# First weight blocks of the MLPs requested ahead of the output projections, second matmul's first transfers behind them, and two ordering choices undone

## The chip, the cores and the metric

The kernel runs on one core of a Trainium2 chip. The core has five engines that run side by side and meet at semaphores: PE (TensorE, matrix products; PEld is its loading of the stationary operand), DVE (VectorE), ACT (ScalarE), POOL (GpSimd) and SP (SyncE, which here only issues DMA transfers). Transfers between the main memory and the on-chip memory are issued by SP and, where they accumulate into their target, by POOL; each of the two issues in the order of its own queue. The metric is the device time of one execution in microseconds (us).

## The reference: what is computed

Two encoder layers on x of 512 tokens by 1024 features, float32. Each layer is a token mixer and a dense MLP, each behind an RMS norm and added to the residual:

```python
def sq_relu_mlp(h, w1, w2):
    a = jax.nn.relu(h @ w1)
    return (a * a) @ w2
...
for i in range(DEPTH):                        # DEPTH = 2
    h = rms_norm(x, norm_mix[i])
    y = dilated_mixer(h, ...) if i % 2 == 0 else mla_mixer(h, ...)   # each ends with  o @ w_o
    x = x + y
    h = rms_norm(x, norm_ffn[i])
    x = x + sq_relu_mlp(h, ffn_w1[i], ffn_w2[i])
```

w1 is 1024 by 4096 and w2 is 4096 by 1024. The mixer of layer 1 is a dilated window attention with a joint q/k/v projection, that of layer 2 a latent attention over all positions. Both end with an output projection w_o of 1024 by 1024.

## The kernel before

**Arithmetic.** Float32 operands are split into a rounded high part and a remainder (ACT writes `whi`, DVE subtracts and writes `wlo`), and each product is three matmuls: high by high, high by low, low by high. The large matmuls save products in the manner of Strassen and Winograd: a 2 by 2 block product takes seven products, numbered 1 to 7, of sums and differences of blocks.

**The MLP.** `mlp` works in eight groups of 512 columns of w1 (class `Up`, first matmul) and four chunks of 1024 rows of w2 (`wino`, reached by `down(ch)`, second matmul). A group has four weight blocks of 512 KB. The first, key (0, 0), goes to a tile with the tag `wk` (two slots) when the `Up` is made. `rest()` loads the other three into tiles with the tag `raw` (three slots, which the output projection's weights use as well). `product(p)` makes the high and low part of its weight operand in slots `whi` and `wlo` (four each) and issues 24 matmuls of 128 by 256 at L968. Products 5 and 6 add another block to the first one on DVE (L936, L938). Products 7 and 4 need blocks that an accumulating DMA on POOL has added to (`load(..., add=True)`, L922). The blocks of the normalised activations are written by `project`, in `hT_f` (`H` in `Up`; the order in it is `H_OF`).

`wino` first runs `fetch` for four pairs of half blocks into `wqs`: eight plain loads on SP (L788) and four accumulations on POOL (L786); this is its first `next(d)`. `wqs` takes the place of the attention output that the projection reads. In `mlp` the sequence is: group 0's loads, its products 1 and 2, group 1's product 1, group 0's products 5, 6, 3, 7, 4, group 1's loads and its products 5, 6, 3, 7, 2, 4; then for each chunk the `plan`, in which a 0 stands for `next(d)` and another number for a product of the current group.

**The output projection and the norm.** `project` multiplies the attention output by w_o in two column halves (`run_block` at L185, weights loaded at L147 and split at L157 and L158), adds to the residual (L1077), normalises each of four row tiles (L137, L1051), transposes it on PE (L124) and writes the blocks of `hT_f` with ACT and DVE (L1042, L1043, and sums at L1064 to L1071). It runs in a pool `po` (or `po1`), which is closed before the MLP's pool is opened; `hT_f` stands in an outer pool (`h1`, `bh`).

**Order.** A planner sets the order of the instructions on each engine from the order in which they are written, their dependencies and its own estimate of times, so that a transfer can go ahead of work written before it. `tc.issue_after(ins)` holds everything written in its block behind `ins` on the engine of `ins`. Pools with `reuse_waits="tile"` share memory with closed pools, and a new tile waits for the release of the tiles whose place it takes.

**Two other places.** `v_phase` does the v projection of layer 1 by seven products for each of three head groups. Its `piece(g, ba)` needs the sum bT + b21 for product 4; for g = 0 it is formed by two accumulating DMAs that read the weights again (L464), for the others by `add_block` on DVE (L334). `wq` has six slots for these blocks. In layer 2 the attention runs over four pairs of heads; `score` notes the maximum and the exponential of each step, and the splits of the second w_o on DVE and ACT are held behind the first step of the last pair.

Of the kernel before, what the change touches and what calls it, by code (L numbers as in the profile page):

```python
# [10 lines left out]
F32 = mybir.dt.float32  # L11
# [6 lines left out]
P = 128  # L18
# [69 lines left out]
def encoder_kernel(ctx: ExitStack, tc: tile.TileContext, x, norm_mix, norm_ffn, a_w_qkv, a_q_gain, a_k_gain,  # L88
# [218 lines left out]
    def v_phase(vp):  # L307
# [139 lines left out]
        def piece(g, ba):  # L447

            bb = new_banks("b")
            both(5, bT[g], bb, True)  # L450
            put(g, 1, 1, "set", bb, False)
            add_block(bT[g], bT[g], b22[g])
            both(3, b22[g], bb, False)
            put(g, 0, 1, "set", bb, False)
            b3 = vp.tile([P, 4, VH], F32, tag="h32", name=nm("b3"))
            add_block(b3, b12[g], b22[g])
            both(6, bT[g], ba, False)
            put(g, 0, 1, "sub", ba, True)
            if g:
                add_block(bT[g], bT[g], b21[g])  # L460
            else:

                for u in range(2):
                    nc.gpsimd.dma_start(bT[g][:, 2 * u:2 * u + 2], wblk(g, 1, 0, u), accum_op=ALU.add)  # L464
# [300 lines left out]
    def wino(tag, Aq, w, wqs, asps, pool, resid, done=None):  # L765
# [28 lines left out]
        def sums(p, t):  # L794

            if p == 7:
                if done is None:
                    d = gp.tile([P, 4, 256], F32, tag="gain", name=nm("d"))
                else:
                    d = pool.tile([P, 4, 256], F32, tag="wk", name=nm("d"), bufs=2)  # L800
                V.tensor_tensor(d, Aq(0, 0), Aq(1, 0), op=ALU.subtract)
                split_to(t, d)
            elif p == 6:
                split_to(t, S["d"])
            else:
# [99 lines left out]
    class Up:  # L905
# [3 lines left out]

        CHAIN = {1: "a", 6: "a", 7: "a", 4: "a", 5: "b", 3: "b", 2: "d"}  # L910

        def __init__(self, w1, c0, H, a2, pool):
            self.v = w1.rearrange("(k p) c -> p k c", p=P)
            self.c0, self.H, self.a2, self.banks = c0, H, a2, {}
            self.w = {(0, 0): self.load((0, 0), pool.tile([P, 4, 256], F32, tag="wk", name=nm("wk"), bufs=2))}

        def load(self, key, t, add=False):

            ki, ni = key
            src = self.v[:, 4 * ki:4 * ki + 4, self.c0 + 256 * ni:self.c0 + 256 * ni + 256]  # L920
            if add:
                nc.gpsimd.dma_start(t, src, accum_op=ALU.add)  # L922
            else:
                nc.sync.dma_start(t, src)
            return t

        def rest(self):
# [55 lines left out]
                V.tensor_tensor(c, c, av, op=op)  # L983
                self.end(c, c)

    def mlp(layer, w1, w2, H, resid, pool, done):
        wqs = big.tile([P, 8, 2, 512], F32, tag="hT", name=nm("wqs"))
        asps = pool.tile([P, 2, 4, 2, 256], F32R, name="asp")
        a2c = pool.tile([P, 4, S], F32, name="a2")
# [2 lines left out]
        homes = [a2ab[:, 0], a2ab[:, 1], a2c]  # L992

        def group(h):
            return Up(w1, 512 * h, H, homes[h % 3], pool)

        def down(ch):
            a2s = [homes[(2 * ch + j) % 3] for j in range(2)]
# [2 lines left out]
                        done if ch == 3 else None)  # L1001


        g0 = group(0)
        g0.rest()
        g0.product(1)
        g0.product(2)
        g1 = group(1)
        g1.product(1)
        for p in (5, 6, 3, 7, 4):  # L1010
            g0.product(p)
# [5 lines left out]
        for ch in range(3):  # L1017
            d = down(ch)
            for h, plan in ((2 * ch + 2, (0, 1, 5, 0, 6, 3, 0, 7, 2, 0, 4, 0, 0)),
                            (2 * ch + 3, (1, 5, 6, 0, 3, 7, 2, 0, 4))):  # L1020
                g = group(h)
                g.rest()
                for p in plan:
                    if p:
                        g.product(p)
                    else:
                        next(d)
        for _ in down(3):
# [62 lines left out]
    h1p = tc.tile_pool(name="h1p", bufs=1, reuse_waits="tile")  # L1091
    h1 = h1p.__enter__()
    hT = h1.tile([P, 7, 4, 2, 256], F32R, name="hT_f0")
    with tc.tile_pool(name="po", bufs=1, reuse_waits="tile") as po:
        project(oA, a_w_o[0], resid, norm_ffn[0:1, :].rearrange("o d -> (o d)"), hT, po, "g_ffn0",
                first_cols)
    with tc.tile_pool(name="mlp0", bufs=1, reuse_waits="tile") as mp:
        state = {}

        def done0(r, c):  # L1100
            state[r] = state.get(r, 0) + 1
            if state[r] < 2:
# [10 lines left out]
    if True:  # L1113
        with tc.tile_pool(name="bpool", bufs=1, reuse_waits="tile") as bp, \
# [153 lines left out]
            def score(d, h, r):  # L1268
# [6 lines left out]
                for i, (lt, rt) in enumerate(ops):  # L1275
                    PE.matmul(sc, lhsT=lt, rhs=rt, start=(i == 0), stop=(i == 4))  # L1276
                mx = st.tile([P, 4], F32, tag="bmx", name=nm("bmx"))
                marks["max"] = V.tensor_reduce(mx[:, 0:1], sc, axis=AX.X, op=ALU.max).ins
                V.tensor_scalar(mx[:, 1:2], mx[:, 0:1], rq, -1.0, op0=ALU.mult, op1=ALU.mult)
                pe = bw.tile([P, S], F32, tag="pe", name=nm("pe"), bufs=3)  # L1280
                marks["exp"] = A.activation(pe, sc, AF.Exp, bias=mx[:, 1:2], scale=rq, accum_out=mx[:, 2:3]).ins
# [41 lines left out]
            for s_ in range(HB * NT + lag):  # L1323
                p, c = divmod(s_, 8)
                if s_ < HB * NT:
                    if c == 0 and p:
                        cur = nxt
                    pend.append((cur, c // 4, c % 4, score(cur, c // 4, c % 4)))
                    if s_ == HB * NT - 8:
                        last_pair = marks["max"], marks["exp"]  # L1330
                if s_ >= lag:
                    d, h2, r2, f = pend.pop(0)
                    if r2 == 0:
# [17 lines left out]

    bh = ctx.enter_context(tc.tile_pool(name="bh", bufs=1, reuse_waits="tile"))
    hT = bh.tile([P, 7, 4, 2, 256], F32R, name="hT_f1")

    with tc.tile_pool(name="po1", bufs=1, reuse_waits="tile") as po, \
            tc.issue_after(last_pair[0]), tc.issue_after(last_pair[1]):
        project(oB, b_w_o[0], resid, norm_ffn[1:2, :].rearrange("o d -> (o d)"), hT, po, "g_ffn1")
    with tc.tile_pool(name="mlp1", bufs=1, reuse_waits="tile") as mp:
        mlp(1, ffn_w1[1], ffn_w2[1], hT, resid, mp, lambda r, c: nc.sync.dma_start(
            out_v[:, r, 512 * c:512 * c + 512], resid[:, r, 512 * c:512 * c + 512]))  # L1360


# [30 lines left out]
```

## Time and profile before

| | us |
|---|---|
| median of 3 runs | 1465.89 (1465.11 to 1466.90) |
| the profiled execution's own time | 1464.43 |
| its span (first to last instruction) | 1462.7 |
| PE busy | 1380.8 (94%) |
| DVE busy | 1079.1 (74%) |
| ACT busy | 825.0 (56%) |
| POOL busy | 259.0 (18%) |

The mean granted clock of TensorE is 0.979 of full speed. The rows that the next part shows are of a few kinds. A row of the timeline has the start in us, the duration, the engine, the line of the kernel, the operation, the tile written and the tiles read, their sizes and the count of instructions; in square brackets stands how long the engine was idle before it and what ended that. A row of the waits has the waiting engine and tile, what it waited for, the total in us, the number of times and the longest. A row of the chain of work that ended last has the start, the duration and what. A row of windows has the stretch, its length, then the busy time of each engine with the number of its instructions, the granted clock, the mean busy share of the DMA engines and GB/s.

### The profile page before, as it was taken

The page shows a single profiled execution, that of the slowest core. Times are in us where ns is not written, and L with a number is a line of the kernel's source. Part 1 is how long each engine was busy: PE and PEld are TensorE (multiplying, and loading weights), DVE is VectorE, ACT ScalarE, POOL GpSimd, SP SyncE. Part 2 cuts the span into 40 slices and gives each one's busy share as a digit, 9 for nine tenths or more (in the row PEclk, how much of TensorE's full clock was granted, in tenths as well). Part 3 has the DMA queues.
Part 4 walks back from the last instruction along what each step waited for, and adds up shares of the span by engine and source line. Part 5 has one row for each costly group of instructions (what it writes and reads, how often), then busy time and mean ns, then how long its engine had stood idle before and what let it go on. Part 6 is the DMA issues. An engine that isn't in the chain of part 4 may idle for free.

```text
span 1462.7 us, 21731 instructions
## 1 busy us (share of the span) xinstructions
PE 1380.8 (94%) x8004; PEld 1216.5 (83%) x8004; DVE 1079.1 (74%) x1691; ACT 825.0 (56%) x1730; POOL 259.0 (18%) x274
## 2 busy tenths in 40 slices
PE   7999999999999994999999998999895899999998
PEld 7998888888889983999999886777664898999886
DVE  6886758776787646687878787797746687888876
ACT  5554556454665524665656554776524565656663
POOL 1211112011121001121112121433201111221210
PEclk9999999999999996999999998999998899999999
DMA  9635222323222338788988862200115779889855
GB/s 320 191 118 177 86 75 89 97 87 114 82 83 67 99 113 230 169 187 207 194 212 184 198 144 55 80 30 1 58 58 161 159 185 209 195 191 217 182 130 115
DMA packets 154922, 202.98 MB, mean 139 GB/s; under 512 B 8960, under 2 KB 108544, under 8 KB 154816
## 3 DMA queue, kind: packets, MB, share of 16 engines
q1 hardware_dynamic: 118192, 144.96, 31.0%
q0 software_dynamic: 36624, 56.63, 22.8%
q8 instruction: 63, 1.03, 0.3%
q14 instruction: 43, 0.35, 0.1%
HBM read 193.70 MB, written 7.86 MB: 138 GB/s over the span
## 4 chain that ended last, share of the span: by engine, by line
PE 82%; DMA 7%; DVE 4%; issue 3%; ACT 3%; SPq 1%; POOL 0%; ACTq 0%; DVEq 0%; POOLq 0%
PE acc L185 27%; PE acc L968 19%; PE sc L885 11%; PE tp L885 7%; PE tp L124 3%; DMA wk<-in_ffn_w_dram 3%; PE sc L421 2%; DMA wqs<-in_ffn_w_dram 2%; PE acc L1300 1%; PE acc L1276 1%; PE sc L1194 1%; PE tp L421 1%; PE sco L706 1%; PE sc L592 1%; PE sco L702 1%
## 5 line engine op out<-in xcount | busy, mean ns | idle before, releaser
L185 PE MATMUL acc<-whi,hT 128*128 128x512 f32 (+2 forms) x1216 | 384.2, 390 | 2.2 <-ACT hT L744 1.3
L968 PE MATMUL acc<-hT_f,whi 128*128 128x256 f32 x1792 | 329.0, 286 | 33.8 <-ACT whi L954 32.9
L968 PEld LDWEIGHTS acc<-hT_f,whi 128*128 128x128 f32 x1792 | 285.5, 194 | 39.0 <-ACT whi L954 34.3
L185 PEld LDWEIGHTS acc<-whi,hT 128*128 128x128 f32 x1216 | 225.9, 188 | 41.9 <-ACT hT L744 1.9
L968 PE MATMUL acc<-hT_f,wlo 128*128 128x256 f32 x896 | 254.4, 285 | 0.0
L185 PE MATMUL acc<-wlo,hT 128*128 128x512 f32 (+2 forms) x608 | 235.9, 388 | 0.1
L968 PEld LDWEIGHTS acc<-hT_f,wlo 128*128 128x128 f32 x896 | 173.4, 194 | 0.0
L885 PE MATMUL sc<-whi,asp 128*128 128x512 f32 x512 | 164.4, 392 | 3.2 <-ACT asp L762 2.0
L823 DVE TENSOR_TENSOR wlo<-wqs,whi 128x1024 fp32r<-128x1024 f32 x112 | 136.4, 1228 | 32.4 <-ACT whi L822 32.1
L822 ACT ACTIVATE whi<-wqs 128x1024 fp32r<-128x1024 f32 x112 | 118.2, 1055 | 73.2 <-PE acc L968 37.4
L158 DVE TENSOR_TENSOR wlo<-raw,whi 128x1024 fp32r<-128x1024 f32 (+3 forms) x82 | 94.3, 1160 | 55.5 <-ACT whi L157 55.3
L786 POOL DMA_DIRECT2D wqs<-in_ffn_w_dram x64 | 77.2, 1208 | 319.6 <-DMA wqs<-in_ffn_w_dram 166.8
L185 PEld LDWEIGHTS acc<-wlo,hT 128*128 128x128 f32 x608 | 114.4, 188 | 18.9 <-DVE wlo L158 0.4
L885 PEld LDWEIGHTS sc<-whi,asp 128*128 128x128 f32 x512 | 96.9, 189 | 24.5 <-ACT asp L762 4.7
L157 ACT ACTIVATE whi<-raw 128x1024 fp32r<-128x1024 f32 (+3 forms) x82 | 82.3, 1009 | 57.8 <-PE acc L185 21.9
L885 PE MATMUL tp<-whi,asp 128*128 128x512 f32 x352 | 112.3, 390 | 0.0
L132 POOL TENSOR_TENSOR qrs<-rs_v,nhalf 128x4 f32<-128x4 f32 x48 | 59.3, 1241 | 288.2 <-DVE rs_v L129 239.4
L955 DVE TENSOR_TENSOR wlo<-wk,whi 128x1024 fp32r<-128x1024 f32 x64 | 78.2, 1224 | 38.6 <-ACT whi L954 38.3
L954 ACT ACTIVATE whi<-wk 128x1024 fp32r<-128x1024 f32 x64 | 67.6, 1059 | 67.7 <-DMA wk<-in_ffn_w_dram 30.2
L885 PE MATMUL sc<-wlo,asp 128*128 128x512 f32 x256 | 100.6, 393 | 0.0
L137 ACT ACTIVATE junk<-acc 128x128 f32<-128x128 f32 x192 | 53.2, 277 | 56.8 <-PE acc L185 51.8
L955 DVE TENSOR_TENSOR wlo<-raw,whi 128x1024 fp32r<-128x1024 f32 x48 | 58.6, 1224 | 34.7 <-ACT whi L954 32.4
(258 smaller groups left out, 2604.3 us busy)
## 6 DMA issues: line engine op xcount, KB each, us to landing
wqs<-in_ffn_w_dram SPq DMA_DIRECT2D x80, 512.0 KB, 5.0
wqs<-in_ffn_w_dram POOLq DMA_DIRECT2D x64, 512.0 KB, 6.4
raw<-in_a_w_qkv_dram SPq DMA_DIRECT2D x96, 256.0 KB, 3.2
raw<-in_ffn_w_dram SPq DMA_DIRECT2D x48, 512.0 KB, 5.7
b<-in_a_w_qkv_dram SPq DMA_DIRECT2D x24, 384.0 KB, 5.8
wk<-in_ffn_w_dram SPq DMA_DIRECT2D x16, 512.0 KB, 6.8
raw<-in_ffn_w_dram POOLq DMA_DIRECT2D x16, 512.0 KB, 6.5
wk<-in_ffn_w_dram POOLq DMA_DIRECT2D x16, 512.0 KB, 7.6
```

The costliest lines, as they stand in the source:

```text
L132: G.tensor_tensor(out, v[:, :n], nhalf[:, :n], op=ALU.pow)
L137: A.activation(junk, x, AF.Square, scale=1.0 / math.sqrt(dim), accum_out=out)
L157: A.activation(hi[:, :nk, :n], raw[:, :nk, :n], AF.Copy)
L158: V.tensor_tensor(lo[:, :nk, :n], raw[:, :nk, :n], hi[:, :nk, :n].bitcast(F32), op=ALU.subtract)
L185: PE.matmul(accs[o][:, oc], lhsT=lt, rhs=rt, start=(kt == 0 and p_i == 0 and hv == 0), stop=(kt == total - 1 and p_i == 2), skip_group_che ...
L786: marks["sum"] = nc.gpsimd.dma_start(t, src, accum_op=ALU.add).ins
L822: A.activation(hi, x, AF.Copy)
L823: V.tensor_tensor(lo, x, hi.bitcast(F32), op=ALU.subtract)
L885: PE.matmul(bk[t], lhsT=lt, rhs=rt[:, j], start=(first and k == 0 and i_ == 0), stop=(k == 3 and i_ == 2), skip_group_check=True)
L954: A.activation(hi, x, AF.Copy)
L955: V.tensor_tensor(lo, x, hi.bitcast(F32), op=ALU.subtract)
L968: PE.matmul(acc[:, 256 * o:256 * o + 256], lhsT=lt, rhs=rt, start=(first and o == 0 and k == 0 and i_ == 0), stop=(o == 1 and k == 3 and i ...
```

## The change

1. `Up` is made before `project` for groups 0 and 1 of each MLP, with `wk` in the outer pool, so that the two (0, 0) blocks are requested ahead of the output projection. `wk` of the later groups, and `xn` of the next layer's norm, use the same tiles.
2. The first `next(d)` of chunk 0, which issues the eight plain `wqs` loads, is held on SP behind group 1's last plain load.
3. In the last chunk of layer 1 the difference tile of product 7 moves from a `wk` slot to a `raw` slot.
4. In `v_phase`, g = 0 forms its sum with `add_block` like the others.
5. The splits of the second w_o are no longer held behind the last attention pair.

```diff
@@ piece
-            if g:
-                add_block(bT[g], bT[g], b21[g])
-            else:
-                for u in range(2):
-                    nc.gpsimd.dma_start(bT[g][:, 2 * u:2 * u + 2], wblk(g, 1, 0, u), accum_op=ALU.add)
+            add_block(bT[g], bT[g], b21[g])
@@ wino, sums
-                    d = pool.tile([P, 4, 256], F32, tag="wk", name=nm("d"), bufs=2)
+                    d = wp.tile([P, 2, 512], F32, tag="raw", name=nm("d"), bufs=3).rearrange(
+                        "p k (h n) -> p (k h) n", h=2)
@@ Up
-        def __init__(self, w1, c0, H, a2, pool):
+        def __init__(self, w1, c0, H, pool, a2=None):
...
-                nc.sync.dma_start(t, src)
+                self.last = nc.sync.dma_start(t, src).ins
@@ mlp
-    def mlp(layer, w1, w2, H, resid, pool, done):
+    def mlp(layer, w1, w2, H, resid, pool, hpool, g0, g1, done):
...
-            return Up(w1, 512 * h, H, homes[h % 3], pool)
+            return Up(w1, 512 * h, H, hpool, homes[h % 3])
...
-        g0 = group(0)
+        g0.a2, g1.a2 = homes[:2]
         g0.rest()
         g0.product(1)
         g0.product(2)
-        g1 = group(1)
         g1.product(1)
...
-                for p in plan:
+                for n, p in enumerate(plan):
                     if p:
                         g.product(p)
+                    elif h == 2 and n == 0:
+                        with tc.issue_after(g1.last):
+                            next(d)
                     else:
                         next(d)
@@ layer 1
     hT = h1.tile([P, 7, 4, 2, 256], F32R, name="hT_f0")
+    g0, g1 = (Up(ffn_w1[0], 512 * h, hT, h1) for h in range(2))
     with tc.tile_pool(name="po", bufs=1, reuse_waits="tile") as po:
         project(oA, a_w_o[0], resid, ...)
...
-            norm_tile(r, resid[:, r], state["g"], state["hT"], mp, xn_tag="wk")
-        mlp(0, ffn_w1[0], ffn_w2[0], hT, resid, mp, done0)
+            norm_tile(r, resid[:, r], state["g"], state["hT"], h1, xn_tag="wk")
+        mlp(0, ffn_w1[0], ffn_w2[0], hT, resid, mp, h1, g0, g1, done0)
@@ layer 2 (the notes of max and exp in score, and last_pair, go)
     hT = bh.tile([P, 7, 4, 2, 256], F32R, name="hT_f1")
-    with tc.tile_pool(name="po1", bufs=1, reuse_waits="tile") as po, \
-            tc.issue_after(last_pair[0]), tc.issue_after(last_pair[1]):
+    g0, g1 = (Up(ffn_w1[1], 512 * h, hT, bh) for h in range(2))
+    with tc.tile_pool(name="po1", bufs=1, reuse_waits="tile") as po:
         project(oB, b_w_o[0], resid, ...)
...
-        mlp(1, ffn_w1[1], ffn_w2[1], hT, resid, mp, lambda r, c: ...)
+        mlp(1, ffn_w1[1], ffn_w2[1], hT, resid, mp, bh, g0, g1, lambda r, c: ...)
```

More of the change, by code (lines that the diff above doesn't have):

```diff
@@ L1277, in score @@
                 mx = st.tile([P, 4], F32, tag="bmx", name=nm("bmx"))
-                marks["max"] = V.tensor_reduce(mx[:, 0:1], sc, axis=AX.X, op=ALU.max).ins
+                V.tensor_reduce(mx[:, 0:1], sc, axis=AX.X, op=ALU.max)
                 V.tensor_scalar(mx[:, 1:2], mx[:, 0:1], rq, -1.0, op0=ALU.mult, op1=ALU.mult)
                 pe = bw.tile([P, S], F32, tag="pe", name=nm("pe"), bufs=3)
-                marks["exp"] = A.activation(pe, sc, AF.Exp, bias=mx[:, 1:2], scale=rq, accum_out=mx[:, 2:3]).ins
+                A.activation(pe, sc, AF.Exp, bias=mx[:, 1:2], scale=rq, accum_out=mx[:, 2:3])
                 V.reciprocal(mx[:, 3:4], mx[:, 2:3])
@@ L1328, in encoder_kernel @@
                     pend.append((cur, c // 4, c % 4, score(cur, c // 4, c % 4)))
-                    if s_ == HB * NT - 8:
-                        last_pair = marks["max"], marks["exp"]
                 if s_ >= lag:
@@ L1353, in encoder_kernel @@
     hT = bh.tile([P, 7, 4, 2, 256], F32R, name="hT_f1")
-    with tc.tile_pool(name="po1", bufs=1, reuse_waits="tile") as po, \
-            tc.issue_after(last_pair[0]), tc.issue_after(last_pair[1]):
+    g0, g1 = (Up(ffn_w1[1], 512 * h, hT, bh) for h in range(2))
+    with tc.tile_pool(name="po1", bufs=1, reuse_waits="tile") as po:
         project(oB, b_w_o[0], resid, norm_ffn[1:2, :].rearrange("o d -> (o d)"), hT, po, "g_ffn1")
     with tc.tile_pool(name="mlp1", bufs=1, reuse_waits="tile") as mp:
-        mlp(1, ffn_w1[1], ffn_w2[1], hT, resid, mp, lambda r, c: nc.sync.dma_start(
+        mlp(1, ffn_w1[1], ffn_w2[1], hT, resid, mp, bh, g0, g1, lambda r, c: nc.sync.dma_start(
             out_v[:, r, 512 * c:512 * c + 512], resid[:, r, 512 * c:512 * c + 512]))
```

## The prediction

> **What bounds the kernel now.** I read the page first, then the list of waits, the PE rows around the longest waits, and the DMA queue of SP.
>
> ```profile
> span 1462.7 us, 21731 instructions
> PE 1380.8 (94%) x8004; PEld 1216.5 (83%) x8004; DVE 1079.1 (74%) x1691; ACT 825.0 (56%) x1730; POOL 259.0 (18%) x274
> L968 PE MATMUL acc<-hT_f,whi 128*128 128x256 f32 x1792 | 329.0, 286 | 33.8 <-ACT whi L954 32.9
> ```
>
> PE (TensorE) is busy 94% of the span, so 82 us of it is idle at most. The last line is the first matmul of the MLPs: of 33.8 us of idle time before its 1792 instructions, 32.9 wait for one thing, the rounded weight `whi` that ACT makes at L954. The waits say how often, and what ACT waited for:
>
> ```profile
> PE acc L968 <- ACT whi L954: 32.9, 4, 17.3
> ACT whi L954 <- DMA wk<-in_ffn_w_dram: 30.2, 8, 8.3
> ```
>
> Four waits, the longest 17.3 us: two large ones, one per MLP. The PE rows on both sides of them:
>
> ```profile
> 552.92 1.14 PE L124 MATMUL tp<-ck,xn 128*128 128x128 f32 x8 [2.26 <-ACT h L1059]
> ...
> 555.86 1.93 PE L124 MATMUL tp<-ck,xn 128*128 128x128 f32 x8 [1.79 <-DVE dif L1065]
> 575.13 0.79 PE L968 MATMUL acc<-hT_f,whi 128*128 128x256 f32 x2 [17.34 <-ACT whi L954]
> ...
> 595.21 0.50 PE L968 MATMUL acc<-hT_f,whi 128*128 128x256 f32 x2 [0.21 <-ACT a L977]
> ...
> 1119.48 1.94 PE L124 MATMUL tp<-ck,xn 128*128 128x128 f32 x8 [1.79 <-DVE dif L1065]
> 1136.71 0.80 PE L968 MATMUL acc<-hT_f,whi 128*128 128x256 f32 x2 [15.29 <-ACT whi L954]
> ...
> 1157.93 0.51 PE L968 MATMUL acc<-hT_f,whi 128*128 128x256 f32 x2 [0.67 <-ACT a L977]
> ```
>
> The last transposes of the normalisation end at 557.8 and 1121.4; then PE stands still for 17.34 and 15.29 us. Why is in SP's queue:
>
> ```profile
> 511.42 1.50 SPq L924 DMA_DIRECT2D raw<-in_ffn_w_dram  x2
> 549.82 4.09 SPq L788 DMA_DIRECT2D wqs<-in_ffn_w_dram  x8
> 554.25 2.76 SPq L924 DMA_DIRECT2D wk<-in_ffn_w_dram  x2
> 577.50 11.49 SPq L924 DMA_DIRECT2D raw<-in_ffn_w_dram  x3
> ...
> 1049.49 10.70 SPq L147 DMA_DIRECT2D raw<-in_b_w_o_dram  x5
> 1113.44 3.96 SPq L788 DMA_DIRECT2D wqs<-in_ffn_w_dram  x8
> 1117.50 3.15 SPq L924 DMA_DIRECT2D wk<-in_ffn_w_dram  x2
> ```
>
> `wk`, the block that the first product needs, is asked for at 554.25 and 1117.50, right behind eight `wqs` transfers for the second matmul. The chain that ended last names the same two tiles:
>
> ```profile
> 553.43 13.73 DMA wqs<-in_ffn_w_dram
> ...
> 1118.63 21.74 DMA wk<-in_ffn_w_dram
> ```
>
> **The change part by part.** *First blocks early (both MLPs).* Four `wk` transfers (two groups, two MLPs) move ahead of the output projection. They take no engine time but SP's issue, under 0.5 us each. What it removes is the PE gap, and the slow clock behind it:
>
> ```profile
> 575.00:580.00 5.00, 4.71 (x21) 4.42 (x22) 0.52 0.55 149
> 580.00:590.00 10.00, 10.00 (x86) 10.00 (x85) 1.00 0.60 112
> ```
>
> These are windows over L968 alone (length, PE busy and its matmuls, PEld, granted clock, DMA share, GB/s). After the gap the granted clock is 0.52, then 1.00: 21 matmuls take the 4.87 us from 575.13 to 580, and 21 at the later rate (10/86 = 0.116 us) take 2.43. So 2.4 us more is lost per gap. The Trainium skill, "TensorE: Matmul & The Clock Gate", Part 1, says that an idle TensorE falls to half rate and needs some 3.4 us of sustained work to come back. The trace agrees (0.52 against 1.00); by the page the loss would be an estimated 1.7 us per gap, and the sum 1.4 us smaller.
>
> Gone with the wait: 17.3 + 2.4 + 0.2 (the wait at 595.21) = 19.9 us in the first MLP, 15.3 + 2.4 + 0.7 = 18.4 in the second (its slow start taken as in the first).
>
> *What is late next: DVE.* In the same stretch DVE still builds the blocks of the normalised activations:
>
> ```profile
> 549.80:567.00 17.20, 3.94 (x24) 3.02 (x22) 14.50 (x23) 10.19 (x18) 4.24 (x4) 0.68 0.97 298
> 565.74 0.69 DVE L1043 TENSOR_TENSOR hT_f<-dif,hT_f 128x512 fp32r<-128x512 f32 x1 [0.70 <-ACT hT_f L1042]
> 584.19 1.22 DVE L955 TENSOR_TENSOR wlo<-wk,whi 128x1024 fp32r<-128x1024 f32 x1
> ```
>
> DVE is busy 14.50 of the 17.20 us up to 567 (third figure with a count), so 2.7 us are free, and its last block (row at 565.74) ends at 566.4. Products 1 and 2 of group 0 and 1 of group 1 need only blocks of the first two row tiles. They are 3 x 24 matmuls x 0.12 = 8.6 us and carry PE from 557.8 to 566.4. By then DVE must also have done three low parts (row at 584.19, 1.22 us), and for product 5 an addition and a low part of the same size: 6.1 us in 2.7 free ones. So product 5 starts between 566.4 and 566.4 + 3.4 = 569.8; with no row for the order, I take the middle: 1.7 us of new wait. Product 4 needs a DMA accumulation issued after product 6's split; before the change product 7 began 595.21 - 585.41 = 9.8 us after that split and three products hide 8.6, so 0 to 2 us, I take 1. Left: 17.2 and 15.7, together 32.9 us, between 38.3 (no new wait) and 27.5 (both waits at their worst, in both MLPs).
>
> *Second matmul's transfers behind group 1's last load.* The added edge binds only SP's eight `wqs` loads; POOL's four accumulations follow their data. Before the change group 1's loads were issued 577.50 to 589.0, some 14 us after the first product; so afterwards about 560 to 574, and `wqs` from 574. Queued behind it on SP: group 2's blocks. The first product of the second matmul comes after 16 products, 46 us, near 604, so `wqs` has 30 us, and its own lateness costs nothing. But between 560 and 606 the DMA engines must now move 23 transfers of 512 KB (3 of group 1, 8 `wqs`, 4 of group 2, 8 accumulations): 12.1 MB in 46 us, 262 GB/s. Compare:
>
> ```profile
> 575.00:606.00 31.00, 30.50 (x234) 30.01 (x235) 22.31 (x21) 19.41 (x26) 5.15 (x4) 0.92 0.68 143
> raw<-in_ffn_w_dram POOLq DMA_DIRECT2D x16, 512.0 KB, 6.5
> 594.16 1.28 POOL L922 DMA_DIRECT2D raw<-in_ffn_w_dram  x1 [7.17 <-DVE wk L936]
> L954 ACT ACTIVATE whi<-wk 128x1024 fp32r<-128x1024 f32 x64 | 67.6, 1059 | 67.7 <-DMA wk<-in_ffn_w_dram 30.2
> ```
>
> Before the change that stretch ran at 143 GB/s, because the gap had taken the `wqs` traffic; the 298 GB/s at 0.97 share above is near the ceiling. Group 1's first accumulation was issued at 594.16; 6.5 us to land and 2.3 to split (1.06 + 1.22) make it ready at 603, and the product that needs it came five products after 595.2, at 609.6: 6.6 us of slack. Bounds: 0, or 6.5 us per MLP if POOL holds one behind a `wqs` accumulation (rival 1). I take 2 per MLP, nearer 0, since the demand is under the rate shown: 4 us back. The Trainium skill, "DMA: Bandwidth & Descriptors", section "Queues, rings and completion order", says that each DMA engine takes turns between the queues by packet, so a POOL accumulation would not wait out SP's backlog. By that the 4 us would be about 0; no row here separates the two.
>
> *The v stage's block sum on DVE again.* Two accumulating DMAs leave POOL's queue, two DVE additions come.
>
> ```profile
> 51.40 1.23 POOL L464 DMA_DIRECT2D bT<-in_a_w_qkv_dram  x1 [1.37 <-DVE wlo L407]
> 59.25 0.84 ACT L406 ACTIVATE whi<-bT 128x768 fp32r<-128x768 f32 x1 [3.63 <-DMA bT<-in_a_w_qkv_dram]
> 60.88 0.62 PE L421 MATMUL acc<-whi,hT 128*128 128x384 f32 x2 [1.49 <-ACT whi L406]
> 51.62 1.82 DVE L334 TENSOR_TENSOR bT<-b,b 128x768 f32<-128x768 f32 x2
> ```
>
> PE loses 1.49 us to that DMA. The additions cost DVE 1.82 (last row, the same form), in place of that very row: b21 now lives until the additions are done, so the next b11 lands in its slot later and the sum of b11 and b12 at 51.62 must move back. Gain 1.5; if instead the late b11 or DVE holds PE, a loss of up to 1.9. I take the gain, as the DMA wait has its own row.
>
> *The edge on the last attention pair taken back.* The splits of the second w_o may go ahead of the last pair's first maximum and exponential.
>
> ```profile
> 1047.15 2.95 ACT L157 ACTIVATE whi<-raw 128x1024 fp32r<-128x1024 f32 x3
> 1047.31 1.59 PE L1276 MATMUL sc<-kn,qn 128*128 128x512 f32 x3 [2.77 <-ACT pe L1281]
> ```
>
> Earlier splits would let projection matmuls fill the 2.77 us hole (+2.8) or put 2.95 us of ACT work in the way of the softmax (-3.0). I take 0. The difference tile in `raw` and the new home of `xn` change slots that are free by then: 0.
>
> **Sum.** 32.9 - 4.0 + 1.5 = 30.4. The profiled execution took 1464.43 (span 1462.7), so 1434.0; the median of runs is 1.5 above it, so 1435.5 us. Differences under 0.2% (2.9 us) could not be told from none.
>
> **Rivals.**
> 1. *POOL in order.* If the planner sets the `wqs` accumulation before group 1's, POOL waits for its data: six transfers (3.1 MB at 298 GB/s, 10.6 us) after 574, so to 585, two issues of 1.2, then 6.5 to land and 2.3 to split: 596, against a need at 591 (eight products after product 5 at 568.1). With group 1's second accumulation behind it and DVE at its bound, 6 to 7 us per MLP more than I took: 1448. For: the 13.73 us row of `wqs`. Against: from 595 on PE shows no such wait, with the same mix on POOL.
> 2. *Everything fits.* Product 1 also fills the holes before the last transposes (2.26 + 1.79, taken alike in both MLPs: 8.1), no new wait, no crowding: 38.3 + 8.1 + 1.5 + 2.8 = 50.7, 1415. Against: DVE's 14.50 of 17.20.
> 3. *It doesn't do what it says.* `wk` stays late because its place is taken until the projection ends. By the tile sizes it lies behind 56 KB of hT_f, over qkT in layer 1 and vb in layer 2:
>
> ```profile
> L592 PE MATMUL sc<-qkT x32: 270/275/275, 462.5 to 487.0; 128*128 128x128 f32 x32
> 1082.92 3.70 PE L1300 MATMUL tp<-pTs,vb 128*128 128x512 f32 x8 [0.69 <-ACT pTs L1292]
> ```
>
> These end at 487 and 1086.6, 70 and 35 us before the gaps, so little speaks for it: 1464.
>
> 4. *Slower: SP held by the early request.* SP issues in order. Were `wk` set ahead of the five w_o loads of 1049.49, it would hold them until vb is free at 1086.6: 37 us of the second projection, and 1435.5 + 37 = 1472. It decides once the hold passes 30 us. Against: the planner let `raw` go before `wk` at 511.42.
>
> **How the numbers follow.** My forecast 0.57 (its own range 1427 to 1442), rival 1 0.20, rival 2 0.12, rival 3 0.05, rival 4 0.06. The range goes from 1418 (half of rival 2's way) to 1451 (rival 1 with its bounds) and leaves out rivals 3, 4 and part of 2. Faster 0.89, within 0.2% 0.05, slower 0.06.
>
> **What would show it.** Right: no PE wait above 3 us before L968; SP's `wk` rows before the projections' end and `wqs` behind `raw`; a granted clock of 1.0 where 0.52 stood; the first L885 matmul some 17 us nearer to the last transpose. Wrong: waits of PE on `whi` in group 1 with POOL rows idle on DMA wqs (rival 1), or SP idle on PE ahead of L147 (rival 4). The v step is right if the 1.49 us before 60.88 is gone and none came at the next group's start.

## The result and the profile after

The changed kernel takes 1444.62 us (median of 4 runs, 1444.02 to 1446.12), the kernel before 1465.5 beside it (4 runs): the ratio is 0.986, with a 95% interval of 0.984 to 0.988. The gain is 20.9 us; 30.4 were forecast. In the kernel after, L968 has become L964, L954 and L955 are L950 and L951, L885 is L881, L788 and L786 are L783 and L781, L922 and L924 are L918 and L920, and the parts of `hT_f` written at L1042 (ACT) and L1043 (DVE) are now written at L1041 and L1042. The experiments shift the lines again: L966 and L973 below are the same matmul as L964.

The page of the kernel after, its first lines and the group of the MLP's first matmul:

```profile
span 1442.9 us, 21746 instructions
PE 1382.1 (96%) x8004; PEld 1219.4 (85%) x8004; DVE 1081.0 (75%) x1693; ACT 823.3 (57%) x1730; POOL 256.3 (18%) x272
L964 PE MATMUL acc<-hT_f,whi 128*128 128x256 f32 x1792 | 337.9, 290 | 25.6 <-ACT whi L950 12.0
```

PE's work is the same (1382 us), the span 19.8 us shorter. The wait on `whi` has shrunk from 32.9 us to 12.0 and has not gone, and the same 1792 matmuls take 337.9 us where they took 329.0: more of them run at a low clock. PE's rows with a wait above 1 us, first MLP and then second (timeline, in brackets the wait and what ended it):

```profile
553.93 0.58 PE L964 MATMUL acc<-hT_f,whi 128*128 128x256 f32 x1 [2.08 <-DVE hT_f L1042]
568.01 0.38 PE L964 MATMUL acc<-hT_f,whi 128*128 128x256 f32 x1 [2.57 <-ACT hT_f L1041]
569.81 0.38 PE L964 MATMUL acc<-hT_f,whi 128*128 128x256 f32 x1 [1.41 <-DVE hT_f L1042]
607.21 0.80 PE L964 MATMUL acc<-hT_f,whi 128*128 128x256 f32 x2 [6.83 <-ACT whi L950]
609.26 0.58 PE L964 MATMUL acc<-hT_f,wlo 128*128 128x256 f32 x1 [1.25 <-DVE wlo L951]
...
1101.46 0.39 PE L964 MATMUL acc<-hT_f,whi 128*128 128x256 f32 x1 [2.59 <-DVE hT_f L1042]
1115.74 0.38 PE L964 MATMUL acc<-hT_f,whi 128*128 128x256 f32 x1 [2.45 <-ACT hT_f L1041]
1117.51 0.58 PE L964 MATMUL acc<-hT_f,whi 128*128 128x256 f32 x1 [1.39 <-DVE hT_f L1042]
1154.21 0.80 PE L964 MATMUL acc<-hT_f,whi 128*128 128x256 f32 x2 [5.20 <-ACT whi L950]
1156.26 0.58 PE L964 MATMUL acc<-hT_f,wlo 128*128 128x256 f32 x1 [1.25 <-DVE wlo L951]
```

The 17.34 us hole is gone: the first products run from 550.87 us on, between the transposes. The two shorter holes ahead of the transposes (2.26 and 1.79 us) are gone with it. In their place stand two kinds of waits. Three of 1.4 to 2.6 us are for parts of `hT_f`: the one at 553.93 for the second row tile, whose transposes start at 549.58, the two from 565.4 on for the last one, whose transposes end at 564.0. The other kind is one of 6.83 and 1.25 us (5.20 and 1.25 in the second MLP) in group 1, at product 4. The queues show why. SP, then POOL in the first MLP, then the chain that ended last:

```profile
514.95 1.05 SPq L920 DMA_DIRECT2D wk<-in_ffn_w_dram  x2
529.07 40.48 SPq L920 DMA_DIRECT2D raw<-in_ffn_w_dram  x4
569.95 6.85 SPq L783 DMA_DIRECT2D wqs<-in_ffn_w_dram  x8
...
1069.63 0.92 SPq L920 DMA_DIRECT2D wk<-in_ffn_w_dram  x2
```

```profile
592.57 1.18 POOL L781 DMA_DIRECT2D wqs<-in_ffn_w_dram  x1 [9.51 <-DMA wqs<-in_ffn_w_dram]
593.27 1.80 POOL L918 DMA_DIRECT2D wk<-in_ffn_w_dram  x1
```

```profile
575.34 16.69 DMA wqs<-in_ffn_w_dram
...
593.27 11.86 DMA wk<-in_ffn_w_dram
...
605.16 1.06 ACT whi L950
```

SP does what the change says: `wk` at 514.95, `wqs` behind group 1's last load. On POOL an accumulation of `wqs` stands idle 9.51 us for a plain load that took 16.69 us to land, and the accumulation into `wk` that product 4 needs stands behind it in order. Issued at 593.27, it lands 11.86 us later. The clock after such waits, in windows over L964 alone (length, PE, PEld, granted clock, DMA share, GB/s), and a window over all engines for the transfers:

```profile
570.00:575.00 5.00, 5.00 (x31) 5.00 (x31) 0.66 0.85 263
607.00:612.00 5.00, 3.54 (x15) 3.25 (x16) 0.50 0.35 107
```

```profile
576.00:607.00 31.00, 24.39 (x202) 24.08 (x201) 11.68 (x12) 13.27 (x18) 6.10 (x5) 0.96 1.09 273
```

### The profile page after: what moved, and what is told of

It is laid out like the page before. It is cut to its first block, busy times and chain, and to the rows that moved or that the text cites. A ratio compares the mean times of both kernels' runs of the same rounds, so it can differ in the third digit from the quotient of the medians.

```text
span 1442.9 us, 21746 instructions
## 1 busy us (share of the span) xinstructions
PE 1382.1 (96%) x8004; PEld 1219.4 (85%) x8004; DVE 1081.0 (75%) x1693; ACT 823.3 (57%) x1730; POOL 256.3 (18%) x272
## 4 chain that ended last, share of the span: by engine, by line
PE 81%; DVE 7%; DMA 5%; issue 3%; ACT 2%; SPq 1%; POOL 0%; DVEq 0%; ACTq 0%; POOLq 0%
PE acc L185 25%; PE acc L964 18%; PE sc L881 11%; PE tp L881 8%; PE tp L124 4%; DMA wqs<-in_ffn_w_dram 3%; PE sc L421 3%; DMA wk<-in_ffn_w_dram 2%; PE acc L1300 1%; PE acc L1276 1%; PE sc L1194 1%; PE tp L421 1%; DVE wlo L951 1%; PE sco L701 1%; PE sc L587 1%
## 5 line engine op out<-in xcount | busy, mean ns | idle before, releaser
L964 PE MATMUL acc<-hT_f,whi 128*128 128x256 f32 x1792 | 337.9, 290 | 25.6 <-ACT whi L950 12.0
L964 PEld LDWEIGHTS acc<-hT_f,whi 128*128 128x128 f32 x1792 | 291.4, 198 | 31.5 <-ACT whi L950 12.4
L964 PE MATMUL acc<-hT_f,wlo 128*128 128x256 f32 x896 | 257.4, 289 | 2.5 <-DVE wlo L951 2.5
L964 PEld LDWEIGHTS acc<-hT_f,wlo 128*128 128x128 f32 x896 | 176.4, 197 | 3.1 <-DVE wlo L951 3.1
L881 PE MATMUL sc<-whi,asp 128*128 128x512 f32 x512 | 163.4, 390 | 4.5 <-DVE resid L849 2.5
L781 POOL DMA_DIRECT2D wqs<-in_ffn_w_dram x64 | 77.6, 1213 | 334.4 <-DMA wqs<-in_ffn_w_dram 185.3
L881 PEld LDWEIGHTS sc<-whi,asp 128*128 128x128 f32 x512 | 96.2, 188 | 25.6 <-ACT asp L757 6.1
L951 DVE TENSOR_TENSOR wlo<-wk,whi 128x1024 fp32r<-128x1024 f32 x64 | 78.3, 1223 | 46.1 <-ACT whi L950 45.8
L881 PE MATMUL tp<-whi,asp 128*128 128x512 f32 x352 | 112.3, 390 | 0.0
L950 ACT ACTIVATE whi<-wk 128x1024 fp32r<-128x1024 f32 x64 | 67.5, 1058 | 65.0 <-DMA wk<-in_ffn_w_dram 23.9
L881 PE MATMUL sc<-wlo,asp 128*128 128x512 f32 x256 | 99.9, 390 | 0.0
L951 DVE TENSOR_TENSOR wlo<-raw,whi 128x1024 fp32r<-128x1024 f32 x48 | 58.8, 1225 | 36.9 <-ACT whi L950 34.5
```

The lines of the kernel that those rows point to most:

```text
L781: marks["sum"] = nc.gpsimd.dma_start(t, src, accum_op=ALU.add).ins
L881: PE.matmul(bk[t], lhsT=lt, rhs=rt[:, j], start=(first and k == 0 and i_ == 0), stop=(k == 3 and i_ == 2), skip_group_check=True)
L950: A.activation(hi, x, AF.Copy)
L951: V.tensor_tensor(lo, x, hi.bitcast(F32), op=ALU.subtract)
L964: PE.matmul(acc[:, 256 * o:256 * o + 256], lhsT=lt, rhs=rt, start=(first and o == 0 and k == 0 and i_ == 0), stop=(o == 1 and k == 3 and i ...
```

## Where the 20.9 us come from

The same instruction's time in the trace before less that in the trace after places the gain. At the first matmul of `wino` (L885 and L881; 624.1 and 620.2) it is 3.9 us. At product 7's first matmul in the first MLP's last chunk (894.0 and 880.9) it is 13.1. At the first and the last L1300 of attention B it is 11.9 and 17.0 (the last at 1086.0 and 1069.0), and at the second MLP's first `wino` matmul (1186.8 and 1166.8) 20.0. So the two MLP starts, forecast at 32.9, give 3.9 and 3.0, and the rest comes from two places that were costed at nothing: the end of the first MLP (9.2) and attention B (5.1); 1.2 are lost between them.

The end of the first MLP, in PE and DVE of the kernel before, then of the kernel after:

```profile
888.76 1.97 PE L124 MATMUL tp<-ck,xn 128*128 128x128 f32 x8 [5.62 <-DVE xn L220]
891.15 1.22 DVE L801 TENSOR_TENSOR d<-a 128x1024 f32<-128x1024 f32 x1
894.02 1.23 DVE L763 TENSOR_TENSOR asp<-d,asp 128x1024 fp32r<-128x1024 f32 x1 [0.25 <-ACT asp L762]
```

```profile
876.71 1.22 DVE L758 TENSOR_TENSOR asp<-d,asp 128x1024 fp32r<-128x1024 f32 x1
880.94 0.47 PE L881 MATMUL sc<-whi,asp 128*128 128x512 f32 x1 [1.26 <-DVE resid L849]
```

Before, product 7's operand is split at 894.02, since its difference tile waited for a `wk` slot that the next layer's normalised tiles held; PE meanwhile ran their transposes after 5.62 us of standing. After, its last part is made from 876.71 to 877.9, 3 us ahead of the matmul.

## The experiments

All times are medians; the kernel before was run beside each group of them (1464.95 to 1466.94).

**The changed kernel again**, unchanged, as a base for what is changed in it.

> The changed kernel itself, beside the three that follow, so that differences of a few microseconds can be read. 1444.6 us, 0.986 of the kernel before.

Measured: 1444.61 us.

**`wqs` behind product 4's accumulation.** The order of rival 1, turned round: group 1's second accumulation now goes ahead of `wqs`.

```diff
-                nc.gpsimd.dma_start(t, src, accum_op=ALU.add)
+                self.acc = nc.gpsimd.dma_start(t, src, accum_op=ALU.add).ins
...
-                        with tc.issue_after(g1.last):
+                        with tc.issue_after(g1.last), tc.issue_after(g1.acc):
```

> The changed kernel, with the first transfers of the second matmul held until group 1's second accumulating transfer (the one for its product 4) has been issued too; in the changed kernel they are held only until group 1's last plain load has been. Theory A, order on POOL: in the changed kernel that accumulating transfer stands on POOL behind one of `wqs` that waits 9.51 us (first MLP) and 9.53 us (second) for its own data; with the order turned round, TensorE's waits of 6.83 and 1.25 us (first) and of 5.20 and 1.25 us (second) ahead of product 4 go, and with them the slow stretch of clock behind each: 8 to 10 us for each MLP, 16 to 20 together, about 1426 us. Theory B, crowding: the accumulating transfer itself took 11.86 us from issue to landing while the queues moved 273 GB/s; it lands late wherever it stands, and later `wqs` blocks are late instead: a gain of 0 to 4 us, 1441 to 1445.

Measured: 1435.72 us (ratio to before 0.981, 0.979 to 0.982), a gain of 8.9, between the two. PE, DVE and the chain in this kernel:

```profile
605.47 0.80 PE L964 MATMUL acc<-hT_f,whi 128*128 128x256 f32 x2 [3.83 <-DVE a L979]
```

```profile
603.59 1.22 DVE L932 TENSOR_TENSOR wk<-wk,raw 128x1024 f32<-128x1024 f32 x1 [6.89 <-DMA raw<-in_ffn_w_dram]
```

```profile
587.94 15.55 DMA raw<-in_ffn_w_dram
```

The wait at product 4 is gone in both MLPs: the order on POOL made it. A new one of 3.83 us stands close by: group 2's `raw` load takes 15.55 us behind the `wqs` traffic, DVE stands 6.89 us for it, and behind DVE's addition waits the sum from an accumulator that PE needs free. So theory A names the wait, and theory B what is late next.

**Plain `wqs` loads early**, on top of the last kernel: the eight plain loads are asked for right behind group 0's loads, as soon as the projection has released their place (549.56 us), and only the accumulations wait for group 1's.

```diff
+        if tag % 4 == 0:
+            yield         # in wino: the sums are the second next()
...
+        d0 = down(0)
+        next(d0)          # plain loads only
         g0.rest()
...
```

> The kernel of the run in which the second matmul's transfers stood behind product 4's, changed once more: the eight plain `wqs` loads of the first chunk (4 MB) are asked for right behind group 0's loads, and only the accumulating ones wait for group 1's. Theory A, after the order on POOL the queues' room is the bound: there the `raw` load for group 2 took 15.55 us to land behind these loads, VectorE stood 6.89 us for it, and TensorE 3.8 us (first MLP) and 4.6 us (second) behind VectorE, at a clock of 0.55 afterwards. With 4 MB moved into the quiet time ahead of 575 us these waits go: 12 to 15 us less than that kernel's 1435.7, 1421 to 1424 us. Theory B, VectorE or the loads of group 1 (now behind 4 MB more) set the pace: 1432 to 1437 us.

Measured: 1429.14 us (0.976, 0.975 to 0.978), 6.6 less; half of what theory A said. The wait behind DVE falls from 3.8 to 1.4 us (4.6 to 1.2 in the second MLP), and the `raw` load still takes 13 us.

**Sums behind group 2.** An edge on the last plain load of group 2, which was to keep the four sums away from that load:

```diff
-                        with tc.issue_after(g1.last), tc.issue_after(g1.acc):
+                        with tc.issue_after(g.last), tc.issue_after(g1.acc):
```

> The kernel with plain `wqs` early, with the four accumulating `wqs` transfers (2 MB) held until group 2's loads have been issued, and no longer only until product 4's accumulating one has been. Theory A, they still crowd group 2's `raw` load, which took 13.12 us from issue to landing behind them, with VectorE standing 4.60 us for it and TensorE 1.4 us (first MLP) and 1.2 us (second) behind VectorE: with the order turned round these waits and the few microseconds of wqs work that follow go, 3 to 5 us below 1429.1: 1424 to 1426 us. Theory B, the rest of that time is the loads' own, or the accumulating transfers are late for product 5 of the second matmul instead: 1428 to 1434 us.

Measured: 1431.35 us, the same as the last kernel within the intervals (0.9747 to 0.9783 against 0.9747 to 0.9775). The edit was ineffective: the edge acts on the queue of the load it names, SP, and on POOL the four sums stood where they had (issued from 586.78, ahead of group 2's loads). So this run tells nothing of the crowding.

**Sums behind the `raw` load.** The same aim, with an edge on POOL: the plain loads stay early, and the four sums are written just ahead of product 5 of the second matmul and held behind group 2's first accumulation.

```diff
...
+            if tag % 4 == 0 and p == 5:
+                with tc.issue_after(marks["g2"]):      # group 2's first accumulation
+                    fetch(sT, (0, 1), add=True)
+                    fetch(s7, (1, 1), add=True)
...
```

> The kernel with plain `wqs` early, with the four accumulating `wqs` transfers put on POOL behind group 2's first accumulating transfer (at 604.73 us there), so that they cannot crowd the `raw` load that precedes it. Theory A, these 2 MB crowd it: the load lands in 7 to 10 us and not in 13.12, VectorE's wait of 4.60 us and TensorE's of 1.4 and 1.2 us go: 2 to 4 us below 1429.1, 1425 to 1427 us. Theory B, the load's time is that of the plain loads issued with it, or the sums are now late for product 5 of the second matmul (needed at about 622 us, asked for from 605 us): 1429 to 1436 us.

Measured: 1426.31 us (0.973, 0.972 to 0.975), as theory A said. The transfers issued from 586 to 600 us (count, size each, median us from issue to landing) and PE's waits from 575 to 626 us; first the kernel with the sums ahead:

```profile
wqs<-in_ffn_w_dram POOLq DMA_DIRECT2D x4, 512.0 KB, 15.7
raw<-in_ffn_w_dram SPq DMA_DIRECT2D x3, 512.0 KB, 13.1
```

and the one with the sums behind:

```profile
raw<-in_ffn_w_dram SPq DMA_DIRECT2D x3, 512.0 KB, 4.6
```

```profile
PE acc L973 <- DVE hT_f L1051: 0.2, 1, 0.2
```

The three loads land in 4.6 us where they took 13.1, and PE runs from 575.2 to the second matmul with 0.2 us of waits. It is the fastest whole version: 39.6 us under the kernel before beside it and 18.3 under the changed one.

**`wqs` not held**, the changed kernel without its second part:

```diff
-                        with tc.issue_after(g1.last):
-                            next(d)
+                        next(d)
```

> The changed kernel without the edge that holds the second matmul's first transfers: its plain loads then stand on SP's queue between the `raw` loads of group 0 and group 1, and on POOL two of its accumulating transfers stand ahead of group 0's second one. Theory A, order on POOL decides: group 0's accumulating transfer is late too, and TensorE waits 5 to 10 us more in each MLP: 1450 to 1465 us. Theory B, the queues' room decides: the loads use the time in which the changed kernel's queues moved 71 GB/s (545 to 560 us) and have landed when POOL comes to them, so nothing is held: 1435 to 1442 us.

Measured: 1439.57 us (0.982, 0.981 to 0.984), 5.0 less than the changed kernel and inside theory B's range. The hold costs time. Without it the wait moves; PE's row in the first MLP and the chain's piece ahead of it:

```profile
581.92 0.58 PE L964 MATMUL acc<-hT_f,whi 128*128 128x256 f32 x1 [5.12 <-ACT hT_f L1040]
```

```profile
565.25 14.10 DMA raw<-in_ffn_w_dram
```

now for group 1's `raw` load, crowded in its turn at 14.10 us: DVE's addition stands for it, and behind that the part of `hT_f` that PE needs. Theory A's price was wrong; the loads used the quiet time, as theory B says, but not for nothing.

**The difference tile alone**, in the kernel before:

```diff
-                    d = pool.tile([P, 4, 256], F32, tag="wk", name=nm("d"), bufs=2)
+                    d = wp.tile([P, 2, 512], F32, tag="raw", ...)
```

> The kernel before, with one thing of the change: product 7's difference tile of the last chunk lies in `raw` and not in `wk`. Theory A: in the trace before, TensorE waited 5.62 us (at 888.76) at the end of the first MLP while that tile waited for a `wk` slot that the normalised tiles of the next layer held; in the changed kernel the tile was ready 6 us before it was needed, and between the last chunk's first product and the first score behind it 9.4 us were gained. Then this edit alone gives 8 to 9 us: 1456 to 1457 us. Theory B, as the prediction costed it, the tile is worth nothing and the 9.4 us came from the new home of the normalised tiles or from earlier starts: 1464 to 1466 us.

Measured: 1456.41 us beside 1465.28 for the kernel before (0.994, 0.993 to 0.995): 8.9 us for this edit alone, as theory A said. The wait of 5.62 us is gone, and PE's one wait above 1 us at that place is:

```profile
885.12 0.71 PE L886 MATMUL sc<-whi,asp 128*128 128x512 f32 x1 [2.13 <-DVE resid L854]
```

**The edge put back** in the changed kernel:

```diff
-    with tc.tile_pool(name="po1", ...) as po:
+    with tc.tile_pool(name="po1", ...) as po, \
+            tc.issue_after(last_pair[0]), tc.issue_after(last_pair[1]):
```

> The changed kernel with the edge behind the last attention pair put back (the output projection of attention B again starts its transfers behind that pair's maximum and exponential). Theory A, the edge held the splits of `w_o`: in the trace before, three of them stood at 1047.15 us, in the changed one at 1009.41, 1025.45, 1037.65 and 1047.09 us, and attention B with its last pair gained 5.1 us between the first score of layer 1 and the last normalised tile; with the edge back that is lost, 1448 to 1450 us. Theory B, as the prediction took it, the edge cost nothing and the 5.1 us came from another shift: 1443 to 1446.

Measured: 1449.31 us (0.990, 0.989 to 0.991), 4.7 more, inside theory A's range. ACT and PE with the edge:

```profile
1035.38 2.95 ACT L157 ACTIVATE whi<-raw 128x1024 fp32r<-128x1024 f32 x3
1035.54 0.96 PE L1276 MATMUL sc<-kn,qn 128*128 128x512 f32 x3 [2.76 <-ACT pe L1281]
```

The three splits at one place and the 2.76 us hole are back, as in the trace before. Without the edge the splits lie apart (two of the four up to 1050 us) and PE has no wait there:

```profile
1009.41 1.09 ACT L157 ACTIVATE whi<-raw 128x1024 fp32r<-128x1024 f32 x1
1025.45 1.11 ACT L157 ACTIVATE whi<-raw 128x1024 fp32r<-128x1024 f32 x1
```

**The two small edits together**, in the kernel before, with none of the early requests: the two diffs above, the second one reversed.

> The kernel before with the two small edits together and none of the early requests: product 7's difference tile in `raw`, and no edge behind the last attention pair. If they add up (8.9 us alone, 4.7 us alone), 1451 to 1453 us, and the early requests with the new home of the normalised tiles are worth 6 to 8 us of the whole change. If the one works only with the early requests: 1456 us or more.

Measured: 1454.36 us beside 1466.11 (0.992, 0.991 to 0.994): 11.8 us, between the two ranges. They add up roughly: over the tile alone the edge gives 2.0 us by the medians and 2.8 by the ratios, less than the 4.7 of the changed kernel. What is left for the early requests, the hold and the new home of `xn` is 1454.4 - 1444.6 = 9.8 us, or 8.2 by the ratios.

**The v stage's sum by DMA again**, in the changed kernel:

```diff
-            add_block(bT[g], bT[g], b21[g])
+            if g:
+                add_block(bT[g], bT[g], b21[g])
+            else:
+                for u in range(2):
+                    nc.gpsimd.dma_start(bT[g][:, 2 * u:2 * u + 2], wblk(g, 1, 0, u), accum_op=ALU.add)
```

> The changed kernel with the first group's sum in the v stage taken back to two accumulating transfers. Theory A, from the trace after: the transfers' 1.49 us wait is back, and the 1.42 us for which TensorE waited on VectorE there goes, so that the end of the stage stays: within 1 us of the changed kernel. Theory B, the prediction's term: 1.5 us slower.

Measured: 1444.51 us, no difference. The wait that the addition brings stands in the changed kernel,

```profile
56.90 0.41 PE L421 MATMUL sc<-whi,Ssp 128*128 128x384 f32 x1 [1.42 <-DVE vo L440]
```

and with the DMA sum PE has this row instead:

```profile
59.82 0.62 PE L421 MATMUL acc<-whi,hT 128*128 128x384 f32 x2 [0.80 <-ACT whi L406]
```

**Without the weights' sums on DVE**, in the kernel with plain `wqs` early and, later, in the one with the sums behind the `raw` load:

```diff
-            if p == 5:
+            if p == 5 and self.c0 >= 1024:
                 V.tensor_tensor(T, T, w[0, 1], op=ALU.add)
-            if p == 6:
+            if p == 6 and self.c0 >= 1024:
                 V.tensor_tensor(T, T, w[1, 1], op=ALU.add)
```

> The same kernel as plain `wqs` early, with the four VectorE additions of weights left out in groups 0 and 1 of each MLP (products 5, 6, 3, 7 and 4 of these groups then use unsummed weights; four times 1.22 us of VectorE in each MLP). Theory A, VectorE sets the pace of the MLP's start: from 550 to 576 us it was busy 24.45 of 26 us in the changed kernel, and TensorE waited there 2.08, 2.57 and 1.41 us for VectorE's and ScalarE's parts of `hT_f`; at least the two additions that lie in that stretch ahead of the last part come off: 2.5 to 5 us for each MLP with the slow clock behind the waits, 5 to 10 us below plain `wqs` early. Theory B, the row tiles' own chain (transpose, copy, difference, part) sets it: 0 to 2 us.

Measured: 1436.66 us, 7.5 more with four additions per MLP left out, which neither theory said. The waits for `hT_f` at the start stay (6.2 us in place of 6.3), but group 2's `raw` load takes 15.65 us (13.12 before) and PE waits 3.9 us behind DVE where it waited 1.4.

> The kernel with the sums behind the `raw` load (1426.3 us), with the four VectorE additions of weights left out in groups 0 and 1 of each MLP as in the earlier run of that kind (the products that use them then have unsummed weights). There it made the kernel 7.5 us slower, with group 2's `raw` load at 15.65 us; here that load is no longer crowded. Theory A, the crowding was what made that run slower and VectorE does not set the pace of the start: 1424 to 1428 us. Theory B, VectorE does set the pace and the crowding only hid it: 1416 to 1422 us. Theory C, without the additions the start itself is slower (a lower granted clock where TensorE's waits come earlier): 1430 us or more.

Measured: 1422.46 us (0.970, 0.968 to 0.971), 3.9 less than the kernel it is made from; between the ranges of A and B, and nothing of C. So with the crowding gone, what slowed the earlier run is gone too. The waits at the start are again the same, 6.3 us against 6.2. By the second matmul's first product in the first MLP 3.4 of the 3.9 us are there (606.3 against 609.7), and with waits alike they come from the clock. PE's row in this kernel and the window over L973 that follows:

```profile
552.79 0.39 PE L973 MATMUL acc<-hT_f,whi 128*128 128x256 f32 x1 [1.50 <-DVE hT_f L1051]
```

```profile
552.00:556.00 4.00, 2.77 (x21) 2.56 (x21) 1.00 1.04 379
```

and in the one with the additions:

```profile
553.01 0.39 PE L973 MATMUL acc<-hT_f,whi 128*128 128x256 f32 x1 [2.08 <-DVE hT_f L1051]
```

```profile
553.00:557.00 4.00, 3.81 (x21) 3.52 (x21) 0.67 1.03 354
```

The same 21 matmuls take 2.77 us at 1.00 and 3.81 at 0.67. Behind the next two waits it is the same: 35 matmuls in the 7.4 us from 565.6 at a clock of 0.77 without the additions, 25 in the 7.6 us from 567.4 at 0.55 with them. DVE's sums do not set the length of the waits; that their absence is the cause of the better clock isn't shown.

## Why the prediction was right or wrong

**The first blocks early and what crowds them: 32.9 - 4.0 = 28.9 us forecast, 6.9 measured.** The hole itself went as said; what was set against it failed. In the first MLP, up to the second matmul, the forecast leaves 17.2 - 2 = 15.2 us and the traces give 3.9. The 11.3 between them are three terms.

*Product 4's wait* is the first step that failed: 1 us for it and 2 for the crowding were forecast, 6.83 + 1.25 = 8.1 came (6.5 in the second MLP). The run with `wqs` behind product 4's accumulation shows why: with the order on POOL turned round, it goes. That is 5.1 of the 11.3.

*The clock* is the second: 2.4 us were taken off for the slow stretch behind the old hole, and nothing was set for new ones, although there are three of them (0.66 and 0.50 in the windows above, and the stretch from 553.93). PE's waits fall by 7.4 us from 545 to 626 us (from 21.8 to 14.4), but only 3.9 of these are gained; the 3.5 between lie in the matmuls' own time. So this term is off by 5.9 us, the largest part.

*DVE's parts* cost about what was forecast, though not in the way that was said. The forecast kept the old holes of 2.26 and 1.79 us and added 1.7, together 5.8; in fact product 1 filled the holes, as rival 2 had it, and 2.08 + 2.57 + 1.41 = 6.1 us of waits came. Product 5, forecast to start by 569.8 at the latest, does one matmul at 568.01 and goes on at 569.81. But its price was made up from DVE's additions and low parts, and without the additions the waits stay as they are (6.2 us beside 6.3, and 6.3 beside 6.2).

**Behind group 1's last load: 2 us per MLP forecast.** The hold alone costs 5.0 us, and what it and the crowding keep from the change is 18.3 us (1444.6 against 1426.3), 9 per MLP. The mechanism given for the upper end of this term (6.5) was right, the choice near 0 was wrong, and with the slow clock behind the wait the cost lies above that end. The demand of 262 GB/s came close (273 from 576 to 607 us). The rate of 298 GB/s that it was held against was no ceiling, since a window above shows 379. But the step from "under the rate shown" to "little is late" failed for another reason: the order decides which transfer is late. At that rate the two transfers of 512 KB in the chain take 12 and 17 us, and an engine that issues in order passes the delay on to the next one. The Trainium skill, "DMA: Bandwidth & Descriptors", section "Queues, rings and completion order", has each DMA engine take turns between queues by packet. No run shows the turns themselves. The runs show that loads and accumulations slow each other (a load takes 13.1 us with four sums ahead, 4.6 without; the accumulation for product 4 took 11.86 where the median before was 6.5), so that the conclusion drawn in the forecast, no crowding, doesn't follow.

**Rival 1** is what happened, at the place and with the rows it named (PE on `whi` in group 1, POOL idle on DMA `wqs`). It expected 1448 us; the two small edits, which it too had at nothing, make up for a start that was worse still. The "against" that was held up to it, that no such wait showed before with the same mix on POOL, was weak evidence: there the `wqs` traffic went by in the hole. Rivals 3 and 4 are excluded by SP's rows: `wk` at 514.95 and 1069.63 us, ahead of the projections' end, with the w_o loads issued before it. Of rival 2, product 1 filling the holes came true; the rest would need a start without waits, and even the fastest order keeps 6.2 us there. Of the signs named, `wk` ahead of the projections' end and `wqs` behind `raw` are there. The others are not: in each MLP one PE wait is above 3 us, the clock falls to 0.50 again, and the second matmul's first product is 10.1 us nearer to the last transpose (56.2 in place of 66.3) where 17 were named, 6.2 of them only because the transposes now end later.

**The two terms of nought.** The difference tile was "slots that are free by then": 8.9 us. The 5.62 us row ahead of 888.76 was in the trace before and was not read; it lies more than 300 us behind the MLP's start. The edge was taken at 0 between +2.8 and -3.0; it is 2.0 to 4.7.

**The v stage: 1.5 us forecast, 0 measured.** The other bound of that term came true in part: DVE, now with two additions more, holds PE 1.42 us at 56.90 for the 1.49 us gone at 60.88.

So errors on both sides partly cancelled: some 22 us too much for the MLP starts with their crowding, 1.5 too much for the v stage, 11 to 14 too little for the two small edits. That 1444.62 lies within 1418 to 1451 is therefore in good part luck; it is outside the forecast's own range of 1427 to 1442 and nearer to rival 1. (Half the way from 1435.5 to rival 2's 1415 is 1425, not the 1418 at which the range begins; nothing hangs on it here.)

## What to carry to other kernels

A transfer asked for earlier is worth the hole that it closes less everything that it then stands in front of: list, for each queue that issues in order, which waiting instruction comes ahead of the one that the critical engine needs next, and put the needed one first. Before a tile's new home is costed at nothing, look for who waits for the old slot anywhere in the kernel. A wait of 2 us on TensorE is to be costed with the slow stretch that may follow it.

## What was not expected of the hardware

The granted clock fell after waits much shorter than thought: 2.08 us at 553.93, and a window of 0.50 behind 2.59 us in the second MLP of the fastest whole version. The Trainium skill, "TensorE: Matmul & The Clock Gate", Part 1, gives about 3.4 us of idleness for that; these runs do not agree. Nor is there a sharp bound in them. Of two waits of 1.5 us at the same matmul, the one shown above was followed by a clock of 1.00; the other, in the first kernel without the weights' sums, has this row and this window over L966:

```profile
552.93 0.58 PE L966 MATMUL acc<-hT_f,whi 128*128 128x256 f32 x1 [1.52 <-DVE hT_f L1046]
```

```profile
553.00:557.00 4.00, 4.00 (x19) 4.00 (x20) 0.50 1.04 379
```

The same part of the page says that the clock watches a free-running window of activity, so that the point of change varies from run to run; that would fit, and no run here tests it.

Plain 512 KB loads that land in 4.6 us (median of three) took 13.1 when four accumulating ones of that size had been issued just ahead.
